# Attention's output projection by seven half-width products, fifteen pairs of convolution products joined by accumulating transfers, and a written order of jobs

## The chip, the cores and the metric

The kernel runs on one core of one Trainium2 chip. That core has five engines with instruction streams of their own: TensorE (PE, matrix products into PSUM banks), VectorE (DVE), ScalarE (ACT), GpSimd (POOL) and SyncE (SP); here POOL and SP only issue transfers. The metric is device time in microseconds (us). The median of three runs of the kernel before is 895.05 us (895.77, 894.91, 895.05).

## The reference

One layer of a hybrid block on 512 positions of 1024 channels, in fp32. Of it, what the change touches:

```python
h = _rmsnorm(x, norm_mix_g)
proj = h @ w_in                       # all three branches and their gates
...
u, ug = jnp.split(p_b, 2, axis=-1)
u = u * jax.nn.sigmoid(ug)
u = _causal_dwconv(u, conv_b_w) + conv_b_bias          # 31 taps
u = jax.nn.silu(_layernorm(u, ln_b_g, ln_b_b))
y_b = u @ w_b_out
...
o = jnp.einsum("bhsm,bmhd->bshd", pr, vh).reshape(bsz, seq, D_ATT)   # 4 heads
y_c = o @ w_att_out
g = jax.nn.sigmoid((p_g + b_gate).reshape(bsz, seq, N_BRANCH, D_MODEL))
merged = g[:, :, 0] * y_a + g[:, :, 1] * y_b + g[:, :, 2] * y_c
return merged @ w_o
```

Behind it come a residual sum, a feed-forward layer with a three-tap convolution, and a last norm.

## The kernel before

**Products.** Each fp32 operand is split in a high part (rounded by an ACT copy: `whi`, `oh`, `fb00h`) and a low part (the rest, by a DVE subtraction: `wlo`, `ol`, `fb00l`), and each product is three matmuls: high by high, high by low, low by high. Weights come in units of 128x1024: `fetch_job` loads one by SP into a slot of the `wf` ring, `split_job` has job `wh` (ACT, L649) make the high part and `wl` (DVE, L653) the low part. For a few units the low part is made by ACT (a negated copy, L668) and an accumulating GpSimd transfer from memory (L670) instead.

**Seven products.** Most projections are cut into 2x2 blocks and done by seven block products in place of eight. `quad_loads` fetches four blocks of weights (`u`, `v`, `s`, `r`) and has GpSimd form their sums and differences by accumulating transfers from memory (L773; jobs `s5`, `s6`, `s7`, `s3`). `form_jobs` makes sums and differences of the activations' blocks on DVE (`t5`, `t7`, `t6`, `t4`) and their high and low parts (`fh` on ACT, `fl` on DVE). `multiply` does product `f`, 24 matmuls of 128x256 (L819), into one of three PSUM banks, and `quad_reads` takes the banks out: ACT copies `r1`, `r2`, `r5`, `r6`, `r4`, DVE adds `r7`, `r3` (L864).

**Attention's projection.** The four heads' outputs are taken from PSUM as `oh` (ACT, L1360) and `ol` (DVE, L1365), 128x512, eight times each. `pe_merge(2, m)` multiplies them by eight weight units, 24 matmuls of 128x512 each (L1649 to L1651, 192 in all), and the job `weigh` (DVE, L1684) multiplies each bank by its gate, `("g", 2, m)`. Branches 0 and 1 have the same code and keep it.

**The long convolution.** Branch B's 31 taps run over four tiles `p` of 256 channels (128x2x512). For 23 of the 30 shifts `s` ACT multiplies the input by the tap's weight into a tile `tp` (L1465, job `tp`) and DVE adds it to `acc` (L1472, job `tap`); for the other seven DVE does both (L1457). The taps of one tile are a chain on `acc`, and all are spread beside PE's products until the layer norm of branch B, which needs them.

**What sets the order.** PE's order is written. For the others the class `Jobs` plans: each job has a cost, what it comes after and which slots it takes (rings `wf`, `sb`, `lf`, `ps`); latest starts are worked back from PE's order, shifted by the tables `LATER` and `AHEAD`, and `run` picks the job that can start first, then the one due first. `issue_in_program_order` makes each engine issue in that order. Waits on data stay semaphores. `wait_for` lets a transfer wait for an instruction of another engine as well.

Of the kernel before, what the change touches and what calls it, by code (L numbers as in the profile page):

```python
# [14 lines left out]
P = 128  # L15
# [41 lines left out]
SOON = 8.0  # L57
# [9 lines left out]
ACT_TAPS = [s for s in range(1, 31) if s % 4]  # L67
UNIT_BUFS = 4
# [5 lines left out]
SUMS_BY_VECTOR = [("glu", 0)]  # L74

LATER = {
    "ACT c3": -79.87, "ACT cf": -109.54, "ACT csq": -49.02, "ACT exp": -408.18,
# [3 lines left out]
    "ACT mg": -6.51, "ACT mgh a": -131.92, "ACT mgh b": -203.04, "ACT mgh c": -161.97,  # L83
    "ACT mgh d": -323.72, "ACT mgh e": -90.58, "ACT mgh f": 308.75, "ACT mgh g": -153.29,
    "ACT msq": 15.04, "ACT mu high": -0.01, "ACT oh": -226.41, "ACT pth": -176.82,
# [12 lines left out]
    "ACT table end": -197.25, "ACT table exp": 5.67, "ACT table gates": 1.59,  # L98
    "ACT table glu": -252.31, "ACT table last": -0.01, "ACT table silu": -28.73,
    "ACT table swish": -15.77, "ACT table v": -32.24, "ACT table x": -1.37, "ACT tap 0": -202.88,  # L100
    "ACT tap 1": 192.35, "ACT tap 2": 130.71, "ACT tap 3": 262.1, "ACT tp 0": 393.84,
# [9 lines left out]
    "ACT xroot": -17.08, "ACT xsq": 6.07, "ACT xsquare": -30.79, "ACT zh a": -613.81,  # L111
    "ACT zh b": -91.24, "ACT zh d": -69.92, "ACT zh e": -4.53, "ACT zh f": -126.12,
    "ACT zh g": -8.78, "DVE CV": -695.74, "DVE c3": -191.73, "DVE centre": 202.15,
    "DVE cf": 294.92, "DVE csum": -277.07, "DVE ends": -149.6, "DVE fl h b00": 0.11,
# [6 lines left out]
    "DVE low": 2.25, "DVE m fold": 28.63, "DVE m scale": 0.66, "DVE mg": -19.19,  # L121
    "DVE mgl a": -285.28, "DVE mgl b": 9.87, "DVE mgl c": 24.34, "DVE mgl d": -328.43,
    "DVE mgl e": 5.19, "DVE mgl f": -202.26, "DVE mgl g": 30.97, "DVE ml": -162.14,
    "DVE ms c": 28.78, "DVE ms d": -34.22, "DVE ms e": -158.41, "DVE ms f": -32.65,
    "DVE msum": 21.9, "DVE mu fold": -34.05, "DVE mu low": -5.13, "DVE mu sum": -94.23,
    "DVE ol": -0.27, "DVE ones": 10.22, "DVE pn": -16.92, "DVE ptl": 12.87, "DVE ql": -416.07,
# [8 lines left out]
    "DVE tap 0": -146.19, "DVE tap 1": -22.08, "DVE tap 3": 883.23, "DVE top": -136,  # L135
    "DVE tot2": 9.06, "DVE um": -21.63, "DVE v scale": -87.66, "DVE var fold": -166.47,
# [10 lines left out]
    "DVE xn": 252.5, "DVE xnorm": 0.88, "DVE xsum": -41.53, "DVE ymul": 451.68, "DVE ys": 77.3,  # L147
# [3 lines left out]
    "NONE mem tile": -421.13, "NONE mg tile": -11.65, "NONE raw tile K": -29.96,  # L151
    "NONE raw tile V": -19.48, "NONE rows": -2.04, "NONE silu": 110.97, "NONE sums": 30.32,
    "NONE temps": -552.42, "NONE z": -444.78, "POOL ea": -162.13, "POOL s3 bb": -417.37,
# [80 lines left out]
def wait_for(tc, ins, other):  # L234
# [5 lines left out]
        reason="paced",  # L240
    )


class Jobs:

    def __init__(self, tc, rings):
# [2275 lines left out]
```

## Time and profile before

| | before |
|---|---|
| median of 3 runs | 895.05 us |
| span of the profiled execution | 894.3 us |
| instructions | 16686 |
| memory read, written | 185.31 MB, 4.19 MB |

The profiled execution is given by its span alone, first instruction to last; it is 0.75 us shorter than the median time. The busy time of an engine counts its instructions without waits. In the groups of instructions a row names line, engine, operation, output and inputs, the count, busy time, the mean of one in ns, and the idle time just before them with its releaser. In a table of windows each engine's busy time in a stretch stands beside its count, then the granted clock of PE, the mean busy share of the 16 transfer engines and their rate.

### The profile page before, as it was taken

What the parts mean: (1) busy time and instruction counts of PE and PEld (TensorE: products, weight loads), DVE (VectorE), ACT (ScalarE), POOL (GpSimd) and SP (SyncE); (2) the same over time, 40 slices, a digit from 0 to 9 for tenths busy, and PEclk for the clock granted to TensorE, in tenths of its full rate; (3) what the DMA queues carried; (4) which work ended last, traced back from release to release, by engine and by line L of the source; (5) the groups of instructions that cost most, each with busy time, mean ns of one, the idle gap of its engine ahead of it and who ended that gap; (6) DMA issues with size and microseconds to landing.
All of it is one profiled execution on the core that took longest, in us unless ns stands there. A gap on an engine that the chain in (4) does not pass through costs nothing.

```text
span 894.3 us, 16686 instructions
## 1 busy us (share of the span) xinstructions
PE 886.0 (99%) x6649; PEld 847.4 (95%) x6649; DVE 822.5 (92%) x928; ACT 677.8 (76%) x933; POOL 126.8 (14%) x153
## 2 busy tenths in 40 slices
PE   9999999999999999999999999999999999999997
PEld 8999999999989999999899988899999999998886
DVE  6997999999989999999897969898999889999997
ACT  7767989989987888787967753776766677875665
POOL 0021121111011121111100011021211121001220
PEclk9999999999999999999999999999999999999999
DMA  9999789767569997988856497499999877779992
GB/s 357 391 256 209 151 196 195 189 138 171 165 161 233 210 212 179 231 190 218 212 111 213 178 337 160 115 236 309 281 239 231 210 163 151 197 261 323 229 220 96
DMA packets 54221, 190.59 MB, mean 213 GB/s; under 512 B 6144, under 2 KB 6528, under 8 KB 54144
## 3 DMA queue, kind: packets, MB, share of 16 engines
q0 software_dynamic: 20880, 75.24, 47.0%
q1 hardware_dynamic: 32976, 114.02, 35.3%
q8 instruction: 52, 0.85, 0.4%
q10 hardware_dynamic: 288, 0.27, 0.1%
q14 instruction: 25, 0.20, 0.1%
HBM read 185.31 MB, written 4.19 MB: 212 GB/s over the span
## 4 chain that ended last, share of the span: by engine, by line
PE 93%; DVE 5%; issue 1%; ACT 0%; DVEq 0%
PE bank L819 57%; PE bank L601 6%; PE bank L602 6%; PE bank L600 6%; PE bank L1649 5%; PE bank L1651 5%; PE bank L1650 5%; PE bank L1153 2%; DVE wlo L653 2%; DVE zl L2197 1%; DVE upc L1598 1%; DVE gtc L1598 1%; PE bank L2014 0%; PE bank L1889 0%; PE bank L1393 0%
## 5 line engine op out<-in xcount | busy, mean ns | idle before, releaser
L653 DVE TENSOR_TENSOR wlo<-wf,whi 128x1024 fp32r<-128x1024 f32 x196 | 235.0, 1210 | 22.6 <-ACT whi L649 22.4
L649 ACT CAST whi<-wf 128x1024 fp32r<-128x1024 f32 x202 | 209.4, 1042 | 60.8 <-PE bank L819 18.8
L1465 ACT ACTIVATE tp<-u,pk 128x511 f32<-128x511 f32 (+22 forms) x184 | 118.8, 705 | 3.1 <-DVE acc L1472 2.5
L1472 DVE TENSOR_TENSOR acc<-acc,tp 128x1022 f32<-128x1022 f32 (+22 forms) x92 | 109.2, 1187 | 6.8 <-ACT tp L1465 5.1
L773 POOL DMA_DIRECT2D wf<-in_w_in x52 | 46.5, 914 | 231.8 <-DVE wlo L653 148.5
L819 PE MATMUL bank<-ft6h,wlo 128*128 128x256 f32 x232 | 64.0, 276 | 1.1 <-DVE wlo L653 1.1
L819 PE MATMUL bank<-fb10h,whi 128*128 128x256 f32 x232 | 64.0, 276 | 0.0
L819 PE MATMUL bank<-fb11h,whi 128*128 128x256 f32 x232 | 64.0, 276 | 0.0
L819 PE MATMUL bank<-ft5l,whi 128*128 128x256 f32 x232 | 63.9, 275 | 0.0
L819 PE MATMUL bank<-fb11h,wlo 128*128 128x256 f32 x232 | 63.9, 275 | 0.0
L819 PE MATMUL bank<-fb00h,whi 128*128 128x256 f32 x232 | 63.9, 275 | 0.0
L819 PE MATMUL bank<-fb00l,whi 128*128 128x256 f32 x232 | 63.9, 275 | 0.0
L819 PE MATMUL bank<-fb00h,wlo 128*128 128x256 f32 x232 | 63.8, 275 | 0.0
L819 PE MATMUL bank<-fb10l,whi 128*128 128x256 f32 x232 | 63.8, 275 | 0.0
L819 PE MATMUL bank<-fb10h,wlo 128*128 128x256 f32 x232 | 63.8, 275 | 0.0
L819 PE MATMUL bank<-ft5h,wlo 128*128 128x256 f32 x232 | 63.8, 275 | 0.0
L819 PE MATMUL bank<-ft6l,whi 128*128 128x256 f32 x232 | 63.8, 275 | 0.0
L819 PE MATMUL bank<-ft7l,whi 128*128 128x256 f32 x232 | 63.8, 275 | 0.0
L819 PE MATMUL bank<-ft7h,wlo 128*128 128x256 f32 x232 | 63.8, 275 | 0.0
L819 PE MATMUL bank<-ft4l,whi 128*128 128x256 f32 x232 | 63.8, 275 | 0.0
L819 PE MATMUL bank<-ft4h,wlo 128*128 128x256 f32 x232 | 63.8, 275 | 0.0
L819 PE MATMUL bank<-fb11l,whi 128*128 128x256 f32 x232 | 63.8, 275 | 0.0
(388 smaller groups left out, 3144.5 us busy)
## 6 DMA issues: line engine op xcount, KB each, us to landing
wf<-in_w_in SPq DMA_DIRECT2D x53, 512.0 KB, 5.2
wf<-in_w_in POOLq DMA_DIRECT2D x52, 512.0 KB, 7.0
wf<-in_w_up POOLq DMA_DIRECT2D x33, 512.0 KB, 8.3
wf<-in_w_up SPq DMA_DIRECT2D x30, 512.0 KB, 7.9
wf<-in_w_down SPq DMA_DIRECT2D x15, 512.0 KB, 4.4
wf<-in_w_att_out SPq DMA_DIRECT2D x8, 512.0 KB, 4.0
wf<-in_w_a_out SPq DMA_DIRECT2D x8, 512.0 KB, 4.4
wf<-in_w_b_out SPq DMA_DIRECT2D x8, 512.0 KB, 5.4
```

The costliest lines, as they stand in the source:

```text
L600: nc.tensor.matmul(ps, s_hi, w_hi, start=start, stop=False, skip_group_check=again)
L601: nc.tensor.matmul(ps, s_hi, w_lo, start=False, stop=False, skip_group_check=again)
L602: nc.tensor.matmul(ps, s_lo, w_hi, start=False, stop=stop, skip_group_check=again)
L649: nc.scalar.copy(parts[0], src())
L653: nc.vector.tensor_tensor(lo, src(), hi.bitcast(F32), op=ALU.subtract)
L773: nc.gpsimd.dma_start(out=tiles[key], in_=block(w, col[c], k), accum_op=ALU.add)
L819: nc.tensor.matmul(ps[:, c, :], w[:, i, at], in_turns(a[i]), start=first and n == 0, stop=i == 3 and n == 2, skip_group_check=again,)
L1465: nc.scalar.activation(two(("tp", p, s))[:, j, s:], two(("u", p))[:, j, : SEQ - s], AF.Copy, scale=weight(j),)
L1472: nc.vector.tensor_tensor(a, a, two(("tp", p, s))[:, :, s:], op=ALU.add)
L1649: nc.tensor.matmul(ps, w_hi[:, i, at], hi, start=first, stop=False)
L1650: nc.tensor.matmul(ps, w_hi[:, i, at], lo, start=False, stop=False)
L1651: nc.tensor.matmul(ps, w_lo[:, i, at], hi, start=False, stop=last)
```

## The change

Three things change.

**1. Attention's projection by seven products.** `OUT_QUADS = (2,)` takes it out of the merge's units. The heads' outputs are copied from PSUM by ACT into four blocks `("ob", 2, i, r)` of 128x1024 (job `oc`, 16 copies of 128x256) in place of `oh` and `ol`. `out_forms` makes seven operands of them with `form_jobs` (four sums, seven high and seven low parts, in slots of the `sb` and `lf` rings) and loads weights for two quads, `("out", 2, 0)` and `("out", 2, 1)`; `pe_out` multiplies, 14 products of 24 matmuls of 128x256, 336 in all; `out_reads` takes the banks out and multiplies by the gates. So 192 matmuls of 128x512 go. Of the eight units before, five had low parts by DVE and three by transfer; of the fourteen now all have them by DVE, and eight have a sum formed by a GpSimd transfer.

**2. Joined taps.** For 15 pairs (tile `p`, shifts `s - 1` and `s` of `PAIRED`), GpSimd adds the product tile of shift `s` to that of the shift before by an accumulating transfer from SBUF to SBUF (job `tj`), and DVE adds the joined tile once. DVE's adds at L1472 go from 92 to 77.

**3. A written order.** The planner, `LATER`, `AHEAD` and the share of the queues are replaced by `PLAN`, a list of all jobs with their slots, and for some transfers a job to wait for; `run` walks it. `LOWS_BY_DMA` (units of quads whose low part comes by transfer) is empty.

In numbers of instructions: PE 192 matmuls less at L1649 to L1651 and 336 more at L819. DVE: 15 tap adds, eight `ol` and eight `weigh` less; nine `wlo`, four sums, seven `fl`, and in `out_reads` four adds and six products of 128x512 and four products of 128x256 more. ACT: eight `oh` and three lowered weights less; six `whi`, seven `fh`, sixteen copies of 128x256 and six copies of 128x512 more. POOL: 15 joins and eight weight sums more, three lowered weights less, 158 to 178 transfers.

```diff
+PAIRED = [(p, s) for p in range(4) for s in (1, 9, 17, 25) if (p, s) != (3, 25)]
...
-LATER = {
-    "ACT c3": -79.87, "ACT cf": -109.54, "ACT csq": -49.02, "ACT exp": -408.18,
...
+OUT_QUADS = (2,)
+LOWS_BY_DMA = []
...
+PLAN = [
+    (("mem tile", 0), "sb12"), (("ldm", 0, 0), ""), (("raw tile", "K"), "wf2"),
...
+    def run(self):
+        assert sorted(map(str, self.jobs)) == sorted(str(key) for key, *_ in PLAN)
...
+        for key, given, *held in PLAN:
+            engine, fn, after, take, use = self.jobs[key]
...
             fn()
             if len(code) > n_code:
...
+                for other in held:
+                    wait_for(self.tc, code[n_code], last[other])
+                last[key] = code[-1]
...
     def seeded(q):
 
-        return q in SEEDED
+        return q in SEEDED or q[0] == "out"
...
+    def out_reads(q, gates, sigmoids):
...
+        def read5():
+            make(y)
+            nc.scalar.activation(parted(right[1]()), turned(view("b")), AF.Copy, scale=-1.0)
+
+        def add(i, b, op):
+            t = parted(right[i]())
+            nc.vector.tensor_tensor(t, t, turned(view(b)), op=op)
+
+        def by_bank(i, b):
+            t = parted(gate[i]()[:, :, lo_t])
+            if i:
+                for j in range(2):
+                    nc.vector.scalar_tensor_tensor(
+                        t[:, j], turned(view(b))[:, j], -1.0, t[:, j], op0=ALU.mult, op1=ALU.mult)
+            else:
+                nc.vector.tensor_tensor(t, turned(view(b)), t, op=ALU.mult)
+
+        def by_tile(i):
+            t = gate[i]()[:, :, hi_t]
+            nc.vector.tensor_tensor(t, t, right[i](), op=ALU.mult)
...
+            def o_block(h=h, d=d, bank=bank):
+                for r in range(2):
+                    blk = ("ob", 2, h // 2, r)
+                    if h % 2 == d == 0:
+                        make(blk)
+                    nc.scalar.copy(
+                        four(blk)[:, 2 * (h % 2) + d, :], turned(tiles[bank])[:, r, :])
...
-            def tap_add(p=p, s=s):
-                a = two(("acc", p))[:, :, s:]
-                nc.vector.tensor_tensor(a, a, two(("tp", p, s))[:, :, s:], op=ALU.add)
+            def tap_join(p=p, s=s):
+                nc.gpsimd.dma_start(
+                    out=two(("tp", p, s - 1))[:, :, s:], in_=two(("tp", p, s))[:, :, s:],
+                    accum_op=ALU.add)
+
+            def tap_add(at, p=p):
+                a = two(("acc", p))[:, :, at:]
+                nc.vector.tensor_tensor(a, a, two(("tp", p, at))[:, :, at:], op=ALU.add)
...
+                if (p, s) in PAIRED:
+                    continue
+                at, joined = s, []
+                if (p, s - 1) in PAIRED:
+                    at, joined = s - 1, [("tj", p, s)]
+                    job(joined[0], "POOL", MORE, tap_join, [("tp", p, at), ("tp", p, s)],
+                        MORE_LATENCY, use=[("tp", p, at), ("tp", p, s)])
+                job(("tap", p, s), "DVE", dve(1024 - 2 * at), lambda at=at, add=tap_add: add(at),
+                    [("tap", p, at - 1), ("tp", p, s)] + joined, use=[("acc", p), ("tp", p, at)])
...
+    def out_forms(br, ready):
+        act = f"o{br}"
+        form_jobs(act, {(i, r): ("ob", br, i, r) for i in range(2) for r in range(2)}, ready,
+                  ((0, 0), (1, 0), (1, 1)))
+        for i in range(2):
+            quad_loads(("out", br, i), W_OUT[br], 512 * i, 512 * i + 256, by_dma=True,
+                       take=("wf+" + ANY, 6))
+            out_reads(("out", br, i), [("g", br, 2 * i + c) for c in range(2)],
+                      [("sigmoid", br, 2 * i + c) for c in range(2)])
+
+    def pe_out(br):
+        for f in (1, 2, 5, 6, 7, 4, 3):
+            for i in range(2):
+                multiply_job(("out", br, i), f, f"o{br}")
...
-        (GATE[2, 1], 3): lambda: [pe_merge(2, m) for m in range(4)],
+        (GATE[2, 1], 3): lambda: pe_out(2),
```

At three places the order of instructions shows it. The first is PE where attention's projection begins, before. `fb11h` and `fb11l` are the parts of an operand of the input projection, `oh` and `ol` those of the heads' outputs.

```order
L819 MATMUL bank_2419<-fb11h_785,whi_2927 128x256
L819 MATMUL bank_2419<-fb11l_786,whi_2927 128x256
L819 MATMUL bank_2419<-fb11h_785,wlo_2928 128x256
L1649 MATMUL bank_3040<-oh_2358,whi_2968 128x512
L1650 MATMUL bank_3040<-ol_2445,whi_2968 128x512
L1651 MATMUL bank_3040<-oh_2358,wlo_2969 128x512
```

The same place on PE with the change, where `fh` and `fl` are the parts of the first operand of the seven products.

```order
L1379 MATMUL bank_2953<-fb10h_543,whi_2809 128x256
L1379 MATMUL bank_2953<-fb10l_544,whi_2809 128x256
L1379 MATMUL bank_2953<-fb10h_543,wlo_2810 128x256
L1379 MATMUL bank_3000<-fh_2960,whi_2957 128x256
L1379 MATMUL bank_3000<-fl_2961,whi_2957 128x256
L1379 MATMUL bank_3000<-fh_2960,wlo_2958 128x256
```

The 128x512 matmuls have become 128x256 ones from the same line as the input projection, and a product of that projection (`cv`) now stands ahead of the first.

The second is DVE at the first taps of the first tile, before; `acc` is the sum, `tp` a product that ACT made.

```order
L653 TENSOR_TENSOR wlo_1127<-('glu', 1)_88_516,whi_1126 128x1024
L1472 TENSOR_TENSOR acc_1062<-acc_1062,tp_1097 128x2x511
L1472 TENSOR_TENSOR acc_1062<-acc_1062,tp_1130 128x2x510
L653 TENSOR_TENSOR wlo_1164<-wf_606,whi_1163 128x1024
L1472 TENSOR_TENSOR acc_1062<-acc_1062,tp_1167 128x2x509
L653 TENSOR_TENSOR wlo_1196<-wf_702,whi_1195 128x1024
L1457 SCALAR_TENSOR_TENSOR acc_1062<-u_718,pk,acc_1062 128x508 x2
```

And with the change:

```order
L1200 TENSOR_TENSOR wlo_1188<-wf_926,whi_1187 128x1024
L1200 TENSOR_TENSOR wlo_1218<-('glu', 3)_120_717,whi_1217 128x1024
L2104 TENSOR_TENSOR acc_1055<-acc_1055,tp_1085 128x2x511
L2104 TENSOR_TENSOR acc_1055<-acc_1055,tp_1222 128x2x509
L2084 SCALAR_TENSOR_TENSOR acc_1055<-u_847,pk,acc_1055 128x508 x2
L1425 TENSOR_TENSOR ug_1053<-ug_1053,bank_778 128x2x256
L2104 TENSOR_TENSOR acc_1055<-acc_1055,tp_1257 128x2x507
```

The add of shift 2 (128x2x510) is gone; shift 1's add (128x2x511) now takes both and stands behind a transfer.

The third is GpSimd's queue at the same place, with the change (before it holds only loads from memory there, at L773).

```order
L1329 DMA ('glu', 1)_71_425<-in_w_in 128x1024
L1329 DMA wf_926<-in_w_in 128x1024
L2098 DMA tp_1085<-tp_1122 128x2x510
L1329 DMA wf_660<-in_w_in 128x1024
L1329 DMA ('glu', 3)_120_717<-in_w_in 128x1024
```

The join of shifts 1 and 2 stands between weight sums, in the order of the queue.

More of the change, by code (lines that the diff above doesn't have):

```diff
@@ L253, in __init__ @@
         self.tc = tc
-        self.jobs, self.place, self.left = {}, {}, {}
-        self.rings = {r: {i: 0.0 for i in range(n)} for r, n in rings.items()}
-        self.at, self.work = 0.0, {"SP": 0.0, "POOL": 0.0}
-        self.written = set()
+        self.jobs, self.place, self.rings = {}, {}, rings
         self.first = []
@@ L324, in partly @@
-    def partly(self, name):
-        return name[0] in ("ss", "rows") or name[1] in ("warm", "end")
-    def free_places(self, ring, leave=0):
-        ring, _, whole = ring.partition("=")
-        own, _, other = ring.partition("+")
-        own, other = (
-            [(at, r, i) for r in rs.split() for i, at in self.rings[r].items()
-             if not whole or i in self.written]
-            for rs in (own, other)
-        )
-        return sorted(own + (other if len(other) > leave else []), reverse=True)
@@ L340, in moved @@
-    def moved(self, queue, start):
-        share = SHARE if queue == "SP" else 1.0 - SHARE
-        mine, other = self.work[queue], self.work["POOL" if queue == "SP" else "SP"]
-        if other == 0.0:
-            return start + mine
-        both = min(mine / share, other / (1.0 - share))
-        return start + both + mine - both * share
-    def transfer(self, queue, start, cost):
-        work, t = self.work, self.at
-        share = {"SP": SHARE, "POOL": 1.0 - SHARE}
-        while t < start and (work["SP"] > 0.0 or work["POOL"] > 0.0):
-            both = work["SP"] > 0.0 and work["POOL"] > 0.0
-            rate = share if both else {"SP": 1.0, "POOL": 1.0}
-            step = min([start - t] + [work[q] / rate[q] for q in work if work[q] > 0.0])
-            for q in work:
-                work[q] -= rate[q] * step if work[q] > 0.0 else 0.0
-                if work[q] < 1e-9:
-                    work[q] = 0.0
-            t += step
-        self.at = start
-        work[queue] += cost
@@ new lines, in add, with places @@
+        self.jobs[key] = (engine, fn, list(after), list(take), list(use))
+    def places(self, key, given):
+        for (name, ring, *_), at in zip(self.jobs[key][3], given, strict=True):
+            r = at.rstrip("0123456789")
+            self.place[name] = r, int(at[len(r) :])
+            assert r in ring.replace("+", " ").split("=")[0].split(), (name, ring, at)
+            assert self.place[name][1] < self.rings[r], (name, at)
+            yield name
+    def run(self):
+        assert sorted(map(str, self.jobs)) == sorted(str(key) for key, *_ in PLAN)
+        done, last, left, holder = set(), {}, {}, {}
+        for _, _, _, take, use in self.jobs.values():
+            for name in [name for name, *_ in take] + use:
+                left[name] = left.get(name, 0) + 1
+        for key, given, *held in PLAN:
+            engine, fn, after, take, use = self.jobs[key]
+            assert done.issuperset(after), (key, [k for k in after if k not in done])
+            for name in self.places(key, given.split()):
+                assert not left.get(holder.get(self.place[name]), 0), (key, name)
+                holder[self.place[name]] = name
@@ L453, in run @@
-            ends[key] = free[e] + latency
-            for k in dict.fromkeys(users.get(key, ())):
-                waits[k] -= 1
-                ready_at[k] = max(ready_at.get(k, 0.0), ends[key])
-                if not waits[k] and self.jobs[k][0] != "PE":
-                    ready.setdefault(self.jobs[k][0], {})[k] = ready_at[k]
-            for name in names:
-                left = self.left[name]
-                left[0] -= 1
-                left[1] = max(left[1], ends[key])
-                if not left[0]:
-                    ring, i = self.place[name]
-                    self.rings[ring][i] = left[1]
@@ L466, in run @@
-            n -= 1
+                for other in held:
+                    wait_for(self.tc, code[n_code], last[other])
+                last[key] = code[-1]
+            for name in [name for name, *_ in take] + use:
+                left[name] -= 1
+            done.add(key)
 @with_exitstack
@@ L745, in parts @@
                 after = after + MEM_LAST[key]
-            job(("fh", act, key), "ACT", actv(1024), lambda: high(key, src), after, use=use)
+            own = form_names(act, key)
+            job(("fh", act, key), "ACT", actv(1024), lambda: high(key, src), after, use=use,
+                take=[(n, ANY) for n in own])
             job(("fl", act, key), "DVE", dve(1024), lambda: low(key, src), [("fh", act, key)],
-                use=use)
+                use=use + own)
         before = []
@@ L776, in quad_loads, with whole @@
         fetch_job(v, block(w, col0, 1), after=after, take=take)
[L777 to L778 removed]
+        def whole(f, key, c, k):
+            split_job((q, f), key, 4, 256, [("ld", key)],
+                      lo_from=block(w, col[c], k) if (q, f) in LOWS_BY_DMA else None)
+        whole(1, u, 0, 0)
+        whole(2, v, 0, 1)
         fetch_job(s, block(w, col1, 0), after=after, take=take)
@@ L835, in multiply_job @@
         pe((q, f), 24 * MM_QUAD, lambda: multiply(q, f, act), after,
-           take=[(bank, "ps")] if new else [], use=[] if new else [bank], unit=unit)
+           take=[(bank, "ps")] if new else [],
+           use=form_names(act, OPERAND[f]) + ([] if new else [bank]), unit=unit)
     form_ready = {}
@@ L1368, in o_low @@
                 )
+            def o_block(h=h, d=d, bank=bank):
[5 more added lines that the diff above has]
+                        four(blk)[:, 2 * (h % 2) + d, :], turned(tiles[bank])[:, r, :])
+            if 2 in OUT_QUADS:
+                blks = [("ob", 2, h // 2, r) for r in range(2)]
+                job(("oc", h, d), "ACT", 2 * actv(256), o_block,
+                    [("o", h, d)] + ([("oc", h - h % 2, 0)] if h % 2 or d else []),
+                    take=[(b, ANY) for b in blks] if h % 2 == d == 0 else [],
+                    use=[bank] + (blks if h % 2 or d else []))
+                continue
             job(("oh", h, d), "ACT", actv(512), o_high,
@@ L1662, in pe_merge, with weighed_by @@
                use=parts + (banks if g else []))
+    def out_forms(br, ready):
[11 more added lines that the diff above has]
+                multiply_job(("out", br, i), f, f"o{br}")
+    def weighed_by(br, m):
+        if br in OUT_QUADS:
+            q = ("out", br, m // 2)
+            return [("by4", q), ("by7", q)] if m % 2 else [("by2", q), ("by3", q)]
+        return [("weigh", br, m, j) for j in range(2)]
+    if 2 in OUT_QUADS:
+        out_forms(2, {(i, r): [("oc", 2 * i + h, d) for h in range(2) for d in range(2)]
+                      for i in range(2) for r in range(2)})
     for br in (2, 0, 1):
@@ L1680, in hybrid_block_kernel @@
                 + [("ldp",), ("table", "last" if (br, m) in LAST_GATES else "gates")], use=[gate])
-            for j in range(2):
+            for j in range(0 if br in OUT_QUADS else 2):
                 def weigh(j=j, br=br, m=m, gate=gate):
@@ L1689, in hybrid_block_kernel @@
                     use=[gate, ("bank", "y", br, m, j)])
-            weighed = [("weigh", br, m, j) for j in range(2)]
+            weighed = weighed_by(br, m)
             if br == 0:
@@ L1693, in hybrid_block_kernel @@
                     lambda gate=gate, m=m: add_into(("g", 2, m), gate),
-                    weighed + [("weigh", 2, m, j) for j in range(2)], use=[gate, ("g", 2, m)])
+                    weighed + weighed_by(2, m), use=[gate, ("g", 2, m)])
             elif br == 1:
```

343 lines of the change are left out of this document (152 added, 191 removed), and 836 rows, old and new, of tables (AHEAD, LATER, PLAN).

## The prediction

> **What bounds the kernel now.** I read first the page's busy times and the chain that ended last, then what the tensor engine waited for.
>
> ```profile
> span 894.3 us, 16686 instructions
> PE 886.0 (99%) x6649; PEld 847.4 (95%) x6649; DVE 822.5 (92%) x928; ACT 677.8 (76%) x933; POOL 126.8 (14%) x153
> PE 93%; DVE 5%; issue 1%; ACT 0%; DVEq 0%
> PE bank L819 <- DVE wlo L653: 1.1, 1, 1.1
> PE bank L2014 <- DVE ones L2017: 1.1, 1, 1.1
> PE bank L601 <- DVE wlo L653: 0.7, 1, 0.7
> ```
>
> PE is busy 99% of the span and makes 93% of the chain. All that it waits for besides is 2.9 us in three waits, one of them (1.1 us) at the start. So the kernel is as long as its list of matmuls, and a change pays if it shortens that list while VectorE (DVE), 92% busy, keeps the weight halves `wlo` coming. The profiled execution has a span of 894.3 us, 0.75 under the median of 895.05; I sum against 894.3 and add 0.75 back.
>
> ```profile
> core 0: us, PE busy (x) PEld busy (x) DVE busy (x) ACT busy (x) POOL busy (x), PEclk, DMA share, GB/s
> 75.00:425.00 350.00, 350.00 (x2914) 343.56 (x2913) 336.13 (x373) 302.17 (x448) 52.08 (x60) 1.00 0.82 190
> 234.30:275.70 41.40, 41.40 (x194) 36.25 (x193) 36.89 (x40) 35.40 (x52) 6.04 (x7) 1.00 0.75 177
> 425.00:500.00 75.00, 75.00 (x486) 69.57 (x485) 64.13 (x68) 59.61 (x79) 6.91 (x8) 1.00 0.66 166
> DVE acc L1472 <- ACT tp L1465: 5.1, 5, 1.7
> DVE g L1684 <- PE bank L1651: 3.6, 2, 1.9
> DVE u L864 <- PE bank L819: 3.2, 1, 3.2
> DVE wlo L653 <- ACT whi L649: 3.2, 8, 1.0
> ```
>
> These are windows of the stretches that the change touches (the second is the old attention merge alone) and the largest waits of DVE from 75 to 460 us. From 75 to 425 us, where the taps of the long convolution run, PE never pauses and DVE idles 350.00 − 336.13 = **13.9 us**; from 425 to 500 us it idles 10.9. That is all the slack the change can draw on. The granted clock is 1.00 throughout, so clock plays no part.
>
> **The product itself.** The next rows come from the chain in order of time: start, duration, count.
>
> ```profile
> 234.27 0.22 PE bank L1649
> 275.71 150.08 PE bank L819 x1344
> ```
>
> The attention merge is 192 matmuls of 128x512 between 234.27 and 275.71: 41.44 us, 0.2158 each. Directly behind stand 1344 of the 128x256 kind that the change uses, in 150.08 us, 0.1117 each. Two units of seven products are 14 × 24 = 336 of these: 336 × 0.1117 = 37.5 us. **PE loses 41.44 − 37.52 = 3.92 us.** As half-width matmuls cost a little over half, seven eighths of the work takes 0.905 of the time. Nothing else on PE's list changes in number.
>
> The Trainium skill (TensorE: Matmul & The Clock Gate, Back-to-back issue gap) gives an isolated gap of N/2.4 + 2.5 ns, so 215.8 and 109.2 ns; by it the saving would be 41.4 − 36.7 = 4.7 us. The trace agrees for 512 columns and has 111.7 ns for 256; the measurement decides, and the sum keeps 3.92.
>
> **VectorE's bill.** Durations overlap, so I take start-to-start times from the timeline of DVE.
>
> ```profile
> 345.84 1.15 DVE L1472 TENSOR_TENSOR acc<-acc,tp 128x964 f32<-128x964 f32 x1
> 346.92 1.21 DVE L653 TENSOR_TENSOR wlo<-wf,whi 128x1024 fp32r<-128x1024 f32 x1
> 348.05 1.21 DVE L1574 TENSOR_TENSOR yal<-ya,yah 128x1024 fp32r<-128x1024 f32 x1
> 349.19 1.21 DVE L653 TENSOR_TENSOR wlo<-wf,whi 128x1024 fp32r<-128x1024 f32 x1
> 351.46 0.67 DVE L864 TENSOR_TENSOR C<-C,bank 128x512 f32<-128x512 f32 x1
> 352.06 1.21 DVE L653 TENSOR_TENSOR wlo<-('bb', 1)_553_4187,whi 128x1024 fp32r<-128x1024 f32 x1
> ```
>
> A 128x1024 operation costs 1.135 (346.92 to 349.19, two of them), a 512-column one 0.60 (351.46 to 352.06), a tap add of 964 columns 1.08. Removed: 15 tap adds of some 1000 columns at 1.11 (16.7 us), eight `ol` and eight `weigh` at 0.60 (9.6). Added: nine `wlo` at 1.135 (10.2; fourteen units where five were lowered on DVE and three by transfer), four sums and seven `fl` for the forms of o (12.5), ten reads and weighings of 512 columns (6.0) and four half-width ones at an estimated 0.40 (1.6). The sum is +30.3 − 26.3 = **+4.0 us on DVE**. The joins thus do not relieve DVE; they pay for most of the forms. The stretch shrinks by 3.9 and the work grows by 4.0, so of 13.9 us of idle some **6.0** stay.
>
> Inside the block the new work on DVE (14 `wlo`, 11 for forms, 14 reads) is about 36 us in 37.5, so taps that ran beside the merge move elsewhere. Its cover is the order: the forms' high and low parts are made ahead of the first product, and of the reads PE waits only for those that free a bank, as in the other seven-product units, of which 1344 matmuls ran with no wait. Without that cover, a start that waits for a sum, its high and its low costs about 3 × 1.1 = 3.3 us; I take 0.2, nearer to the row without waits, and keep 3.3 for the range.
>
> ```profile
> L649 ACT CAST whi<-wf 128x1024 fp32r<-128x1024 f32 x202 | 209.4, 1042 | 60.8 <-PE bank L819 18.8
> L1360 ACT CAST oh<-bank 128x512 fp32r<-128x512 f32 x8 | 4.7, 591 | 2.0 <-PE bank L602 2.0
> ```
>
> ACT gets seven form casts and six weight casts at 1.04, six copies of 512 columns at 0.59 and sixteen of 256 at an estimated 0.35, and loses eight `oh` at 0.59 and three lowered weights at about 1.04: some **15 us more**. It idles 350.00 − 302.17 = 47.8 us in the taps' stretch, so I cost it at nothing; without that room it would be late by the part that doesn't fit, and the products of taps with it.
>
> **The joins.** Fifteen times GpSimd issues a transfer that adds one product tile to another in SBUF; the DVE add behind it then waits for a landing. No such transfer ran before. Nearest rows: GpSimd's loads and its accumulating transfers from memory (KB each, median us to landing; the last two rows are those of 75 to 450 us), and the page's queue.
>
> ```profile
> wf<-in_w_in POOLq DMA_DIRECT2D x52, 512.0 KB, 7.0
> wf<-in_w_up POOLq DMA_DIRECT2D x33, 512.0 KB, 8.3
> wlo<-in_w_att_out POOLq DMA_DIRECT2D x3, 512.0 KB, 7.3
> wlo<-in_w_a_out POOLq DMA_DIRECT2D x3, 512.0 KB, 8.1
> q0 software_dynamic: 20880, 75.24, 47.0%
> ```
>
> A join moves 510 KB or a little less, so I bound its landing by 7.0 and 8.3 us. The written order puts between a join and its add two products of PE four times, three seven times, four three times and five once; a product is 24 × 0.1117 = 2.68 us, so the leads are 5.4, 8.0, 10.7 and 13.4 us. At 7.0 us four adds come 1.6 late, 6.4 us in all, which the 6.0 of idle cover but for 0.4. At 8.3 it is 4 × 2.9 + 7 × 0.3 = 13.7, of which 7.7 reach PE. I take 7.0 to 7.3, the rows of loads and of accumulations in the same stretch, and with the forms' 0.2 count a few tenths on PE; both ends stay in the range (0.4 and 7.7 us; a gain is excluded, as the saved adds are in DVE's sum already). What is queued behind such an add on DVE is the next `wlo`, for which PE waits, and the next taps.
>
> The transfers themselves: q0 carried 144 half-megabyte moves in 47.0% of 894.3 us, 2.92 us of the 16 engines each. Twenty more (fifteen joins, eight accumulations for the units' weights, less three lowered weights) are +58 us, nearly all from 75 to 425 us, where the share is 0.82: 287 + 58 = 345 of 346 us.
>
> ```profile
> 350.00:375.00 25.00, 25.00 (x226) 25.00 (x225) 24.89 (x27) 19.96 (x30) 5.21 (x6) 1.00 1.02 226
> 600.00:625.00 25.00, 23.93 (x212) 23.62 (x211) 22.43 (x26) 15.74 (x21) 4.31 (x5) 1.00 1.04 298
> ```
>
> The share is no ceiling in itself: at 1.02 PE ran all 25 us, and at 1.04 the engines moved 298 GB/s, while the new load is about 10.5 MB in 350 us, 30 GB/s on 190. Hence nothing for it, though it may push landings towards 8.3.
>
> **Sum:** 894.3 − 3.92 + 0.35 = 890.7, and 0.75 more is **891.5 us**.
>
> **Rivals.** *Late joins (slower).* Mechanism: the accumulating transfer lands behind the add that wants it, DVE stands, and its queue of `wlo` reaches PE late. Place: the fifteen adds from 75 to 425 us. Price: 15 × mean delay, less the 6.0 of idle. With 8.3 us, 890.4 + 7.7 + 0.75 = **898.8**; with 9.0, 21.4 − 6.0 = 15.4 and 906.5. It passes 896.8 from a landing of about 8.1 us on. For it: a reading and a writing side both in SBUF that no row shows, GpSimd's queue, in which a join stands behind loads that wait for free buffers, and the share near 1.0. By that last, if all landings grow as the load does, 345/287 × 7.0 = 8.4 us, 4 × 3.0 + 7 × 0.4 − 6.0 = 8.8 lost and 900.0. Against it: the full window above, where PE lost nothing, and that most leads exceed 7.3. The Trainium skill (DMA: Bandwidth & Descriptors, Issuing engines are not separate DMA queues) says that all transfers interleave on the same 16 engines whoever issues them, which speaks for this rival; the share of 1.02 without a PE wait does not bear out that it costs anything here. The same page (Anatomy of one DMA — SWDGE (gpsimd) path) has 2.0 us plus bytes/436e3, by which a join would take an estimated 3.2 us and none would be late; the rows' 7.0 to 8.3 do not agree, and they decide.
>
> *Partly given back.* Taps leave the block and the written order puts them later; branch B's normalisation ends the taps, and it is a chain of dependent steps.
>
> ```profile
> 481.85 0.18 DVE L1021 RECIPROCAL cols<-cols 128x4 f32<-128x4 f32 x1 [0.83 <-ACT cols L1018]
> 485.42 1.23 DVE L653 TENSOR_TENSOR whol<-wf,whoh 128x1024 fp32r<-128x1024 f32 x1 [3.39 <-ACT whoh L649]
> ```
>
> DVE idles there in pieces (0.83, 3.39) because others are waited for, so its 10.9 us are not all usable. By the order, priced as above, about 6 us more of DVE work than before stand ahead of this chain; if a third to nearly all of that reaches PE, 2 to 5 us, the time is **893 to 896**. Against it: PE is fully busy in that window, with gate products as cover.
>
> *Better.* The 1.1 and 0.7 us waits for `wlo` in the middle go too, since the new list orders those jobs anew: 890.4 − 1.8 + 0.75 = **889.4**. The start's 1.1 stays. The change not doing what it says (half-width products no faster in this place) would need PE to wait for operands, which is the case "partly given back"; the 0.1117 held over 1344 in a row.
>
> **How the numbers follow.** Forecast, 890.5 to 892.7: 0.49. Better: 0.10. Partly given back: 0.22, a quarter of it under 893.3. Late joins: 0.19, a little of it under 896.8. A measurement of this kernel can tell about 0.2%, 1.8 us, so the bounds are 893.3 and 896.8. Faster: 0.49 + 0.10 + 0.05 = 0.64; same: 0.17 + 0.01 = 0.18; slower: 0.18. The range 889.3 to 897.5 leaves out most of the late joins and a little below, under 2 in 10.
>
> **What would show it.** The 336 products should stand in the chain at 0.112 each, about 37.5 us, with no PE wait inside. DVE busy time should rise by 4 us or so and its idle from 75 to 425 us fall to near 6. The joins' row should show a landing of 7 to 7.5 us, and waits of the tap adds for transfers should sum under 7 us. A landing above 8.1, or waits of PE for `wlo` behind tap adds, makes the forecast wrong by the late joins; PE idle from 425 to 500 us, by the second rival.

## The result, and the profile after

| | before | after |
|---|---|---|
| median | 895.04 us (4 runs, 894.91 to 895.77) | 891.38 us (4 runs, 889.61 to 891.93) |
| span of the profiled execution | 894.3 us | 890.2 us |
| ratio, 95% interval | | 0.9949, 0.9933 to 0.9965 |

Four to five thousandths of the time are gone; the forecast was 891.5 us. A second measurement beside other kernels gave 891.61 us and 0.9953 (0.994 to 0.9965). The profiled execution itself took 891.93 us, so 1.7 us lie around its span.

The page of the changed kernel: its span, the busy times, and the queue that carries GpSimd's transfers (47.0% before).

```profile
span 890.2 us, 17091 instructions
PE 882.4 (99%) x6793; PEld 848.5 (95%) x6793; DVE 823.2 (92%) x931; ACT 686.5 (77%) x957; POOL 149.6 (17%) x173
...
q0 software_dynamic: 25680, 85.53, 53.3%
```

And all that PE waited for (total, times, longest):

```profile
PE bank L1379 <- ACT bank L1413: 1.2, 1, 1.2
PE bank L2681 <- DVE ones L2684: 1.1, 1, 1.1
PE ss L1616 <- DVE msq L1607: 0.2, 1, 0.2
```

PE lost 3.6 us of work (886.0 to 882.4) and 0.4 us of waits (2.9 to 2.5), together the 4.1 us of the span but for rounding. From start to start the 336 new matmuls take 37.6 us with no wait of PE among them, where the 192 old ones took 41.4: this is what the prediction had. DVE's total hardly moved, from 822.5 to 823.2. The joined adds show in the groups of instructions by line:

```profile
L2104 DVE TENSOR_TENSOR acc<-acc,tp 128x1010 f32<-128x1010 f32 (+18 forms) x77 | 91.4, 1188 | 1.7 <-ACT tp L2092 0.6
```

They take 91.4 us where 92 adds took 109.2, and among their idle time there is no transfer. The view of the joins' line says the same from the other side: how long they took to land, and who waited.

```profile
L2098 POOL DMA_DIRECT2D tp<-tp x15: 1205/1205/1209, 88.8 to 431.4; - x15
...
who waited for it (us, times):
  ACT tp L2092: 1.8, 1
  POOL wf L1329: 1.1, 1
...
DMA to landing us min/median/max: 4.8/5.8/8.7
```

A join lands in 5.8 us at the median, sooner than the 7.0 to 7.3 that I took. No DVE add waited for one in this execution. By the order and the trace together the adds start 6.9 to 13.6 us after the join is issued, 0.5 to 8.2 us after it landed. The closest pair, in GpSimd's timeline and then in DVE's:

```profile
413.06 1.21 POOL L2098 DMA_DIRECT2D tp<-tp  x1 [11.44 <-PE bank L1379]
```

```profile
419.95 2.51 DVE L2104 TENSOR_TENSOR acc<-acc,tp 128x1006 f32<-128x1006 f32 x2
```

This join landed after 6.4 us, at 419.4. The prediction's leads counted products of PE between join and add, 5.4 us for the four shortest; the add also stands behind other work on DVE, so the true leads are longer. The margins are thin all the same: in the profile of the second measurement joins landed in 6.1 us at the median, and one add waited 0.5 us.

The stretch that the change touches, in windows, first of the kernel before and then of the changed one:

```profile
core 0: us, PE busy (x) PEld busy (x) DVE busy (x) ACT busy (x) POOL busy (x), PEclk, DMA share, GB/s
75.00:225.00 150.00, 150.00 (x1302) 148.71 (x1301) 143.70 (x175) 135.96 (x215) 21.76 (x25) 1.00 0.77 173
225.00:375.00 150.00, 150.00 (x1166) 144.85 (x1166) 144.21 (x151) 127.75 (x183) 24.28 (x28) 1.00 0.85 200
```

```profile
75.00:225.00 150.00, 150.00 (x1301) 148.71 (x1300) 134.72 (x163) 132.18 (x218) 29.21 (x31) 1.00 0.88 204
225.00:375.00 150.00, 148.85 (x1332) 148.63 (x1331) 147.68 (x158) 131.19 (x185) 36.69 (x40) 1.00 1.02 238
75.00:425.00 350.00, 348.85 (x3072) 347.15 (x3071) 330.52 (x368) 307.62 (x463) 74.70 (x80) 1.00 0.94 222
425.00:500.00 75.00, 75.00 (x482) 69.17 (x481) 71.43 (x74) 64.25 (x87) 8.18 (x9) 1.00 0.70 171
```

From 75 to 425 us DVE idles 19.5 us, more than before (13.9) and far more than the 6.0 predicted, as DVE has less to do there and more behind 425 us, where it went from 64.13 to 71.43. But look where the idle lies: 15.3 us of it ahead of 225 us, and 2.3 us from 225 to 375, where the block and the densest taps are; there the transfer engines are full, too (1.02).

### The profile page after: what moved, and what is told of

It reads as the page before. It is cut to its first block, busy times and chain, and to the rows that moved or that the text cites. A ratio compares the mean times of both kernels' runs of the same rounds, so it can differ in the third digit from the quotient of the medians.

```text
span 890.2 us, 17091 instructions
## 1 busy us (share of the span) xinstructions
PE 882.4 (99%) x6793; PEld 848.5 (95%) x6793; DVE 823.2 (92%) x931; ACT 686.5 (77%) x957; POOL 149.6 (17%) x173
## 5 line engine op out<-in xcount | busy, mean ns | idle before, releaser
L1200 DVE TENSOR_TENSOR wlo<-wf,whi 128x1024 fp32r<-128x1024 f32 x191 | 229.6, 1211 | 11.8 <-ACT whi L1196 11.2
L1196 ACT CAST whi<-wf 128x1024 fp32r<-128x1024 f32 (+1 forms) x194 | 200.2, 1045 | 43.7 <-PE bank L1379 18.5
L2092 ACT ACTIVATE tp<-u,pk 128x502 f32<-128x502 f32 (+22 forms) x184 | 119.0, 709 | 10.4 <-DVE acc L2104 7.5
L2104 DVE TENSOR_TENSOR acc<-acc,tp 128x1010 f32<-128x1010 f32 (+18 forms) x77 | 91.4, 1188 | 1.7 <-ACT tp L2092 0.6
L1329 POOL DMA_DIRECT2D wf<-in_w_in x55 | 50.4, 946 | 178.3 <-DVE wlo L1200 50.6
L1379 PE MATMUL bank<-ft6h,whi 128*128 128x256 f32 x232 | 64.0, 276 | 0.1
L1379 PE MATMUL bank<-ft7h,whi 128*128 128x256 f32 x232 | 63.9, 276 | 0.0
L1379 PE MATMUL bank<-ft4h,whi 128*128 128x256 f32 x232 | 63.9, 276 | 0.0
```

The source lines that it names most:

```text
L1196: nc.scalar.copy(parts[0], src())
L1200: nc.vector.tensor_tensor(lo, src(), hi.bitcast(F32), op=ALU.subtract)
L1329: nc.gpsimd.dma_start(out=tiles[key], in_=block(w, col[c], k), accum_op=ALU.add)
L1379: nc.tensor.matmul(ps[:, c, :], w[:, i, at], in_turns(a[i]), start=first and n == 0, stop=i == 3 and n == 2, skip_group_check=again,)
L2092: nc.scalar.activation(two(("tp", p, s))[:, j, s:], two(("u", p))[:, j, : SEQ - s], AF.Copy, scale=weight(j),)
L2104: nc.vector.tensor_tensor(a, a, two(("tp", p, at))[:, :, at:], op=ALU.add)
```

## Experiments

Ratios are to the kernel before on the same chip, with 95% intervals. Where none is given, the kernel ran once.

### The list of PE

Only `multiply` for attention's quads differs:

```diff
+        if q[0] == "out":
+            starts = f in (1, 5)
+            n_wide = 13 if f in (4, 3) else 14
...
+            for n in range(n_wide):
...
+                nc.tensor.matmul(
+                    tiles[("bank", q, BANK_OF[f])], w[:, n // 3 % 4, at],
+                    in_turns(v[:, h * 512 : (h + 1) * 512]), start=starts and n == 0,
+                    stop=n == n_wide - 1, skip_group_check=not starts)
+            return
```

> The changed kernel, but the fourteen products of attention's projection issue 192 matmuls of 128x512 (ten times 14, four times 13) in place of 336 of 128x256; forms, reads, joins and the written order stay. Attention's projection is not computed (the operands are not those of its product). Theory 'list' (the gain is the shorter list of PE): 891.4 + 41.44 - 37.52 = 895.3 us, between 894.3 and 896.3, and the time of the kernel before is back. Rival 'order' (the gain comes from the new order and the joins, and the list is covered): not above 892.4.

Measured: 894.55 us, ratio 0.9988 (0.9978 to 0.9997). PE's busy time on the page:

```profile
PE 886.4 (99%) x6649; PEld 846.9 (95%) x6649; DVE 823.5 (92%) x931; ACT 685.7 (77%) x957; POOL 149.6 (17%) x173
```

882.4 + 4.0 = 886.4, the predicted 3.92 and within 0.4 of the 886.0 of before; the time rose by 3.2 us, and 894.55 lies in the range of the theory 'list'. With all the rest of the change in place, nearly all of the gain goes with the shorter list. What is left, 0.9988, is about one thousandth.

### What the joins carry

Each product is added by DVE, and the joins are gone from the list; besides, three entries have another slot and one entry another place:

```diff
-                if (p, s) in PAIRED:
-                    continue
-                at, joined = s, []
-                if (p, s - 1) in PAIRED:
...
-                made_taps.append(("tap", p, s))
+                job(("tap", p, s), "DVE", dve(1024 - 2 * s), lambda s=s, add=tap_add: add(s),
+                    [("tap", p, s - 1), ("tp", p, s)], use=[("acc", p), ("tp", p, s)])
+                if (p, s) not in PAIRED:
+                    made_taps.append(("tap", p, s))
```

> The changed kernel without the fifteen joins: each of the thirty products is added by DVE, the two adds of a pair directly behind each other; the rest of the written order stays but for four slots. DVE gets 15 x 1.11 = 16.7 us more. If the joins are what makes room for the seven products' forms (idle of before 13.9, less 3.9, less 20.7 of work), DVE is some 10 us short and the time 899 to 903. If the idle of the changed kernel, 19.5 us from 75 to 425 us and 3.6 from 425 to 500, can be used, 23.1 - 16.7 = 6.4 us are left and the time stays within 891 to 893.5.

Measured: 905.26 us, ratio 1.0117 (1.0099 to 1.0135). DVE's busy time rose by 16.4 us (823.2 to 839.6), and the time by 13.9. Its windows:

```profile
75.00:225.00 150.00, 147.35 (x1265) 144.97 (x1264) 136.47 (x162) 128.27 (x210) 21.73 (x25) 1.00 0.76 174
225.00:375.00 150.00, 146.18 (x1293) 144.87 (x1292) 149.69 (x159) 127.19 (x182) 26.92 (x31) 1.00 0.91 215
```

Between 225 and 375 us DVE is busy 149.69 of 150 and PE loses 3.8 us. Yet between 75 and 225 DVE idles 13.5 us while PE loses 2.7: that idle is DVE waiting for others (6.1 us of it for the high parts that ACT makes), and this order puts no later work there.

The two adds of a pair stand in a row here, which might hold up a weight half at one place. So the same with the first add as early as its inputs allow:

```diff
-    (('tap', 0, 1), ''),
-    (('tap', 0, 2), ''),
...
+    (('tap', 0, 1), ''),
...
+    (('tap', 0, 2), ''),
```

> As without joins, but the first add of each pair stands as early in DVE's order as its inputs allow, up to twelve DVE jobs ahead of the second, in place of directly ahead of it. If the 13.9 us lost without joins are DVE's added 16.7 us of work: 903 to 907 again. If they came from two adds in a row that hold up the weight halves at one place: 891 to 898.

Measured: 906.29 us, ratio 1.012 (1.0106 to 1.0134). So two adds in a row are not the cause, and DVE's added work is what is left.

### What a late join costs

The list gets each join one or two products of PE later, with that product to wait for; the line is one of fifteen:

```diff
-    (("tj", 3, 10), "", (("gate", 0, 1), 7)),
+    (("tj", 3, 10), "", (("gate", 0, 1), 3)),
```

> The changed kernel, but each join waits for one product of PE more, so it is issued some 2.7 us later (1.8 to 4.2). By the margins that the trace shows between a join's landing and its add (0.5 to 8.2 us), DVE then stands 9.1 us in all. If the idle of DVE covers waits (23.1 us), 891 to 893. If waits reach PE one for one, 891.4 + 9.1 = 900.5.

Measured: 905.45 us.

> The changed kernel, but each join waits for two products of PE more, some 5.4 us (4.4 to 7.6); by the margins DVE stands 42.9 us in all. By the prediction's price (the sum of delays less the idle): 891.4 + 42.9 - 23.1 = 911. If one for one: 934. If a stall makes DVE late for the next add, so that the next join is no longer late, less than half of the formula's loss: under 901.

Measured: 951.93 us. The largest waits of DVE in the two, first with one product and then with two:

```profile
DVE acc L3651 <- DMA tp<-tp: 12.4, 7, 3.9
```

```profile
DVE acc L3651 <- DMA tp<-tp: 51.8, 13, 8.4
```

DVE stood 12.4 us for joins, and the time rose by 14.1; it stood 51.8, and the time rose by 60.5. All three expectations for the second run were too low. But DVE was not alone. ACT makes the next product in the tile that a join reads, and it waited for joins as well, again first with one product and then with two:

```profile
ACT tp L3639 <- DMA tp<-tp: 13.1, 4, 4.9
```

```profile
ACT tp L3639 <- DMA tp<-tp: 29.3, 4, 8.5
```

The longest wait of PE in the first of these runs (3.2 us at 105.8 us) was for ACT, which had stood 4.9 us for a join just before. So the runs price late joins as a whole, not the waits of DVE alone. PE's own waits add up to 12.2 and 44 us, where the changed kernel has 2.5: some 10 and 41 us more, about eight tenths of what DVE stood. The idle covers little of it. One part on top has a cause of its own, the granted clock; the mean over the span was 0.997 and 0.983. PE's timeline of the second run behind a wait of 2.51 us:

```profile
422.42 0.38 PE L2926 MATMUL bank<-ft6h,wlo 128*128 128x256 f32 x1 [2.51 <-DVE wlo L2747]
422.63 0.28 PE L2926 MATMUL bank<-ft6h,whi 128*128 128x256 f32 x1
422.75 0.28 PE L2926 MATMUL bank<-ft6l,whi 128*128 128x256 f32 x1
...
423.83 0.42 PE L2926 MATMUL bank<-ft6l,whi 128*128 128x256 f32 x1
424.04 0.42 PE L2926 MATMUL bank<-ft6h,wlo 128*128 128x256 f32 x1
...
427.03 0.30 PE L2926 MATMUL bank<-fb11l,whi 128*128 128x256 f32 x1
427.16 0.28 PE L2926 MATMUL bank<-fb11h,wlo 128*128 128x256 f32 x1
```

From 423.64 to 426.82 us matmuls start 0.21 us apart in place of 0.11. If the clock is half where it is low, a mean of 0.983 over 950 us stands for some 32 us at half speed, an estimated 16 of the 60.5; PE's busy time rose by 18.7 us, from 882.4 to 901.1. A join moved later also moves the weight sums behind it in GpSimd's queue, so part of the rest may be theirs; the runs don't part that.

### The load on the transfer engines

One or two transfers behind each join, from memory to memory:

```diff
+                for n in range(2):
+                    spare = dram.tile([P, 1024], F32, tag=f"spare{p}_{s}_{n}", name=f"spare{p}_{s}_{n}")
+                    nc.gpsimd.dma_start(out=spare, in_=block(w_in, OFF_Q, n))
```

> The changed kernel with one more transfer behind each join on GpSimd's queue: 512 KB from memory to memory, into fifteen tensors that nobody reads. By 2.92 us of the sixteen engines each, the share from 75 to 425 us goes from 0.94 to about 1.05; the joins and weight sums behind them are issued a little over 1 us later at most. If the share is no ceiling (the prediction's view), landings grow by some tenths and the time stays within 891 to 893. If all transfers wait for one another there (the rival), landings grow by a tenth or more, joins with margins of 0.5 to 1.6 us land late, and as waits of DVE reached PE about one for one in the runs with late joins, the time is 895 or more.

Measured with one: 893.92 us, ratio 0.9987 (0.9977 to 0.9996), in ten runs from 891.84 to 896.73. That is 2.5 us more, between the two ranges expected. The profiled execution was the fastest of the ten, yet it shows late joins, contrary to what the next expectation says of it. DVE's wait for them from 75 to 560 us, and PE's longest wait:

```profile
DVE acc L2106 <- DMA tp<-tp: 1.9, 2, 1.7
```

```profile
PE bank L1379 <- DVE u L1425: 1.2, 1, 1.2
```

The join issued at 108.7 us took 10.9 us to land, the add behind it stood 1.7 us, and 8 us later PE waited 1.2 us for DVE. The changed kernel's own wait of 1.2 us at 288 us is absent here, so in this execution the two balance; where the 2.5 us of the median are it cannot say.

> The changed kernel with two transfers of 512 KB from memory to memory behind each join, thirty in all, that nobody reads. One behind each join gave 893.9 (expected: 891 to 893, or 895 and more), though its profiled execution showed no late join. If the load on the sixteen engines costs, the loss grows with it: twice 2.5, so 896 or more, with late landings in the profile. If the 2.5 came from the chip or from the place in GpSimd's queue, 892 to 894.5 again.

Measured with two: 906.44 us, ratio 1.0123 (1.0108 to 1.0139), a loss of 15.1, six times the first and not twice. The profiled execution was again the fastest, 903.26. A wait of ACT from 75 to 460 us, first in the changed kernel and then here:

```profile
ACT whi L1196 <- DMA wf<-in_w_in: 1.0, 1, 1.0
```

```profile
ACT whi L1196 <- DMA wf<-in_w_in: 20.4, 15, 3.0
```

And two of DVE in the same stretch here (7.5 and nothing in the changed kernel):

```profile
DVE wlo L1200 <- ACT whi L1196: 14.0, 20, 2.0
DVE acc L2107 <- DMA tp<-tp: 2.8, 2, 1.7
```

The landing of its weight sums (by GpSimd) and weight loads (by SyncE) from 75 to 450 us (KB each, median us):

```profile
wf<-in_w_in POOLq DMA_DIRECT2D x48, 512.0 KB, 9.9
wf<-in_w_in SPq DMA_DIRECT2D x37, 512.0 KB, 8.1
```

In the second measurement of the changed kernel, on the same chip, in the same stretch:

```profile
wf<-in_w_in POOLq DMA_DIRECT2D x51, 512.0 KB, 7.8
wf<-in_w_in SPq DMA_DIRECT2D x39, 512.0 KB, 6.0
```

SyncE's loads stand in another queue than the added transfers and land later too, so the added load costs, and not only the place in GpSimd's queue. Whether it costs on the engines or in memory, which the added transfers read and write, these runs don't part. The rival was right in its reason and in part in its place: joins come late, but the weight blocks do more so. From load to `whi` on ACT to `wlo` on DVE the waits show the way; PE's own waits here, 10 us in eleven groups, are for several things, 1.7 us of them for `wlo`. The mean share from 75 to 425 us says little of all this: it went from 0.94 to 0.97 and 0.98, where 1.05 was expected with one transfer.

### The old planner, part by part

The parts alone, with the planner and tables of before in place of the list:

```diff
-OUT_QUADS = (2,)
+OUT_QUADS = ()
...
-PLAN = [
+LATER = {
...
+AHEAD = {
```

> The kernel before with its planner and tables and its wide projection, and the fifteen joins alone. DVE has 16.7 us less work than before, PE the same list. If less work on DVE is worth something by itself: at most the 1.8 us of PE's two waits for weights, 893.2. If joins need an order that knows when they land: later than 896.8, since the planner prices a transfer by its own rule and DVE then waits.

Measured: 968.75 us (the diff above is this one; the other has `OUT_QUADS = (2,)` and an empty `PAIRED`).

> The seven products without joins, with the planner, its tables and rules of the kernel before in place of the written order (entries that hold back the forms' parts to 6 us and the new units' loads to 20 us ahead of use are added to the tables, and the new units go by no entry of the old ones). DVE has 20.7 us more than before. If the written order is only a record of what a planner would do, as without joins in the written order: 905. If the order is a condition of its own: 910 or more.

Measured: 927.52 us. Of the joins alone, the largest waits of PE, and DVE's for joins:

```profile
PE bank L835 <- ACT g L895: 24.8, 2, 22.3
PE bank L835 <- DVE wlo L656: 9.7, 5, 5.7
```

```profile
DVE acc L1560 <- DMA tp<-tp: 15.2, 6, 4.5
```

Both are far slower than either kernel (the mean granted clock, 0.967 and 0.983, is part of that), though the joins take work off DVE and the seven products take work off PE. The tables were fitted to the jobs of before, so this shows that the parts don't work in any order that comes, not that no planner could place them.

### A version that goes further

PE's one wait in the middle, 1.2 us, stands behind the seeding copy L1413, and ahead of that copy ACT waited 3.0 us for a weight block that took 9.5 us to land. Two entries change (the rest of their lines is left out):

```diff
-    (("ld", (("cv", 1), "v")), "sb16", ("tap", 1, 26)),
+    (("ld", (("cv", 1), "v")), "sb16"),
-    (("wh", (("cv", 1), 2)), ""),
-    (("r1", ("cv", 1)), "ps7"),
+    (("r1", ("cv", 1)), "ps7"), (("wh", (("cv", 1), 2)), ""),
```

> The changed kernel with two entries of the list moved for the one wait of PE in the middle (1.2 us at 288 us, for the seeding copy of product 2 of the second cv quad): the seeding copy stands ahead of the cast that waits 3.0 us for a weight block, and this block's load no longer waits for a tap. If that transfer's landing of 9.5 us is the cause, PE's wait goes and the time is 890.2 (1.2 less). If something else is next, PE waits elsewhere and it stays at 891.4.

Measured: 889.74 us, ratio 0.9936 (0.9924 to 0.9949). What PE still waits for in all:

```profile
PE bank L2681 <- DVE ones L2684: 1.1, 1, 1.1
```

The wait is gone and none took its place in this execution. The time is 1.6 us under the changed kernel's first measurement, with intervals that overlap, so that the wait went is shown, and the size of the gain isn't resolved.

> The changed kernel unaltered, beside the two below on the same chip: 891.4 us, a ratio of 0.995 to the kernel before, as its first measurement.

Measured: 891.61 us, 0.9953 (0.994 to 0.9965), the second measurement named at the top. Here PE's waits in the middle were shorter:

```profile
PE bank L1379 <- DVE wlo L1200: 0.6, 1, 0.6
PE bank L1379 <- ACT bank L1413: 0.3, 1, 0.3
```

So the wait of 1.2 us in the first profile isn't the same in each execution of the changed kernel, as one would expect of a wait that begins with a transfer's landing.

## Why the prediction was right, and where it wasn't

- **PE's list, 3.92 us less.** Right in mechanism and size: 3.6 us of busy time went, and undoing it alone brought 4.0 us of busy time and 3.2 us of time back. No run shows the forms' 0.2 by itself; PE waited for nothing inside the 336 matmuls.
- **DVE, 4.0 us more.** The busy time rose by 0.7 only, but the bill was nearly right: counts times means of all groups give 883.4 us before and 888.1 after, 4.7 more. Busy time counts an overlap once, and 64.9 us overlap after the change where 60.9 did before, as fewer instructions start behind a pause (140, not 178). The joins do pay for the forms, as the step said: without them 13.9 us are lost.
- **ACT, 15 us more at nothing.** 8.7 measured (677.8 to 686.5), and no loss of PE's in this stretch but the 1.2 us named below.
- **The joins' landing, 7.0 to 7.3 us, and their leads.** 5.8 and 6.1 at the median in the two profiles, with waits of none and 0.5 us. Both errors were on the safe side.
- **"The 6.0 of idle cover" late adds.** This step failed, though nothing in the changed kernel called on it. Its sum was off (19.5 us of idle stayed), but above all little of the idle can be drawn on: 16.4 us of added work cost 13.9, and late joins that held DVE 12.4 and 51.8 us (and ACT beside it) cost 14.1 and 60.5, the slower clock included. Most of the idle lies ahead of 225 us, and DVE is full behind it. The rival's price was therefore too low: with waits at full length, the forecast's distance to 896.8, 5.3 us, is a third of a microsecond of waiting for each join. By the prediction's own leads a landing of 6.7 would have done that (4 × 1.3), not 8.1; that the true leads were longer is what kept it away.
- **Nothing for the transfer engines' share.** It held, but near its edge. Fifteen transfers more cost 2.5 us, thirty 15.1. Signs of it are in the changed kernel already: from 75 to 460 us ACT waits 9.0 us for transfers where it waited 1.5, DVE 7.5 us for ACT's `whi` where it waited 3.2, and PE 1.2 us behind a load of 9.5 us. The forecast of 345 us of load was high: 0.94 of 350 is 329.
- **Partly given back, from 425 to 500 us.** DVE did get 7.3 us more there, as the order said, but PE stayed busy 75.00 of 75.00. The gate products covered it.
- **Better.** Half came true: the two waits of 1.1 and 0.7 us went, and one of 1.2 came. With the entries behind that one changed the time is 889.7, beside 889.4 for this rival.
- **The 0.75 us.** The span came out at 890.2 where the sum had 890.7, and 1.7 us lie around it rather than 0.75. Besides, the profiled execution is 0.55 us above the median. These cancel, so the agreement to a tenth of a microsecond is luck; the steps are good to about one.

## What to carry to other kernels

Where one engine's list bounds the time and a second engine is over nine tenths busy, a shorter list is only as good as the work on the second that pays for it: here 3.9 us of gain stand on some 16 us of work moved to the transfer engines. Price new work or a new wait on such an engine near its full length, from the densest window, and not less the idle of a long stretch. And ask how full the transfer engines are before work is moved to them: at a share of 0.94, fifteen more half-megabyte transfers cost 2.5 us, and thirty 15.

## What had not been expected of the hardware

In the run with joins two products later, a wait of PE of 2.5 us was followed by some 3.2 us in which matmuls of 128x256 start 0.21 us apart, not 0.11, so a stall can cost more than itself. The length of the wait alone does not decide it. In the same run the granted clock fell in the same way behind a wait of 2.4 us (ending at 439.9 us) but stayed at 1.00 behind waits of 3.7 and 3.4 us (ending at 275.4 and 326.6), and the waits of 1.2 us in the changed kernel were not followed by a fall either. What decides is open. The Trainium skill (TensorE: Matmul & The Clock Gate, Part 1: The HAM clock gate (the "warmup" mystery)) tells of such a fall to half clock, after an idle window of about 3.4 us. Here 2.4 us were enough once and 3.7 were not another time; the length of the slow stretch, 3.2 us, is near the page's figure.

The other is the accumulating transfer within SBUF: 5.8 us to landing, under the 7.6 us of GpSimd's weight sums of nearly the same size in the same execution.
